# A two-layer hybrid diffusion block in fp32 on one core: norms split in two steps, and four smaller moves

## The chip, the cores and the metric

One core of a Trainium2 chip runs the whole program in one launch. The metric is the device time of that launch in microseconds (us), the median of the runs that were taken; lower is better. Beside the plain runs there is one profiled execution, from which every view below is read: its engines are PE (TensorE, matrix products), PEld (its weight loads), DVE (VectorE), ACT (ScalarE), POOL (GpSimd) and SP (SyncE, which issues the transfers).

## The reference, cut to what matters

Two layers run over 512 latent tokens (LAT below) and 256 context tokens (CTX). Layer 0 computes both streams; layer 1 needs the context only as keys, values and start states, so most of its products have 512 columns alone.

```python
for l in range(DEPTH):                                   # DEPTH = 2
    need_ctx = l < DEPTH - 1
    mod_l = silu_c @ w_ada[l] + b_ada[l]                 # six (1, 1024) vectors
    sh1, sc1, g1, sh2, sc2, g2 = split(mod_l, 6)         # the same for the context
    h_lat = rms_norm(x, norm1_g[l]) * (1 + sc1) + sh1
    h_ctx = ...
    mix_lat, mix_ctx = token_mixing(h_lat, h_ctx, ...)   # w_in, four branches, gates, w_out
    x = x + g1 * mix_lat
    x = x + g2 * swiglu(rms_norm(x, norm2_g[l]) * (1 + sc2) + sh2, w_ffn_in[l], w_ffn_out[l])
    if need_ctx:
        ...                                              # the same two steps for the context
```

The four branches are a diagonal complex state-space layer (S5), a spatial gating unit (SGU), a Mamba-2 mixer with a short convolution (SSD) and multi-head latent attention (MLA). The sizes that count here: w_out is 1024 x 1024, w_ffn_in 1024 x 5632, w_ada 1024 x 6144, all fp32.

## The kernel before, in words

**Layout.** Activations lie with channels on the 128 partitions and tokens along the free dimension; 1024 channels are eight tiles, numbered k. A projection (`proj`, `mm3`) makes one tile of 128 output channels over one segment of tokens (LAT 512 columns, CTX 256). For every k it runs three products, whi with the low part of the activations, whi with the high part, wlo with the high part: fp32 is split into two fp32r numbers, and 24 products make one output tile.

**Weights.** `weights` fetches 256 columns of a weight (1 MB for 1024 rows) into one of two `raw` buffers, and `wsplit` makes two weight tiles of each: ACT casts `whi`, then DVE or POOL subtracts `wlo`. There are two buffers of each of `whi` and `wlo`. The loop over segments in `layer` stands outside the loop over w_out's tiles, so layer 0 fetches and splits w_out twice, once for LAT and once for CTX; layer 1, with LAT alone, once.

**Norms.** `norm_scale` squares the eight tiles on ACT, adds them on DVE, sums over channels and turns tokens onto the partitions with small products with a matrix of ones, takes 1/sqrt in nine tiny DVE steps (`tok_rsqrt`, `rsqrt`), and spreads the result over the partitions again (`bcast_tok`: DVE scales the identity by it, PE multiplies with ones). `norm_mod` then makes from each tile x the modulated high part h (ACT) and low part (DVE and POOL). It is a generator; one `next` emits a whole segment.

**Order.** The Python code emits instructions in the order of the text, with several generators that are stepped by hand; a list scheduler of the framework then orders every engine's queue by priority and readiness, so an instruction may stand far from where the text has it. Each engine runs its queue in order. SP issues all transfers from one queue.

**The places that the change touches.** (1) The start, in `run`: x, eight chunks of w_ada (`ada_first`) and the context are loaded, then w_in's first columns; the LAT norm, the context's transposes (`turn_x`) and norm, and S5's scalar preparation (`s5_scalars`, DVE) come before layer 0's `mix` starts with the q projections, two tiles (`pair`) over LAT and CTX. (2) `layer`, between w_out and the FFN: after the last w_out tile `next(norm)`, then `late`, three chunks of w_ada (`ada_chunk`: 1 MB each, eight products with 32 output rows, a copy and two transposes), then FFN projections, gate and up. (3) The end of layer 0: the last FFN product is followed by layer 1's first norm (`then`). (4) `prepare`, stepped after each of the 22 hidden tiles of layer 0's FFN: w_ada chunks of layer 1 and S5's matrices for it (`s5_prep`). (5) `mla_pair`, the square sums of q and kv. (6) the callback of the convolution in `mix`.

Of the kernel before, what the change touches and what calls it, by code (L numbers as in the profile page):

```python
# [85 lines left out]
class Net:  # L86
# [194 lines left out]
    def bcast_tok(s, r, nb):  # L281
        dg = s.sc()
        for b in range(nb):
            s.ts(dg[:, b * P:(b + 1) * P], s.ident, r[:, b:b + 1])
        ps = s.b1()
        s.mm(ps[:, :nb * P], s.ones, dg[:, :nb * P])
        return ps
# [111 lines left out]
    def ada_first(s, l):  # L399
# [3 lines left out]
        for pool, tag, c, w, cuts in ((s.hp, "h", 0, 768, (0, 512, 768)), (s.hp, "h", 768, 768, (0, 256, 768)), (s.fp, "f", 1536, 512, (0, 512))):  # L403
            rows = []
            for k in range(KD):
# [5 lines left out]
        return out  # L411
# [74 lines left out]
    def norm_scale(s, xs, off, n):  # L486
# [10 lines left out]
        return s.bcast_tok(s.tok_rsqrt(a, n // P, 1.0 / D, 1e-6), n // P)  # L497

    def norm_mod(s, xs, gs, sh, segs, hh, hl, scaled={}):

        for off, n, v in segs:
            sl = slice(off, off + n)
            if off not in scaled:
                rb = s.norm_scale(xs, off, n)
# [142 lines left out]
    def mla_pair(s, part, q, kd, off, t0, b0, xd, nk, nw, wh, wl, qk):  # L647
# [8 lines left out]
        sq, z = s.sc(), s.sc()  # L656
        s.act(sq, x[:, 0:2].rearrange("p k t -> p (k t)"), AF.Square)
        s.add(sq[:, :256], sq[:, :256], sq[:, 256:])
        if nk == 3:
            s.act(z[:, :256], x[:, 2], AF.Square)  # L660
            s.add(sq[:, :256], sq[:, :256], z[:, :256])
# [623 lines left out]
    def mix(s, l, q, xs, xd, hh, hl, segs, rest, ws):  # L1285
# [92 lines left out]
        def conv(c, segs_):  # L1378
# [3 lines left out]
            def cb(ps, off, n, v):  # L1382
                a = y[:, off:off + n]
                s.act(a, ps, AF.Identity, scale=w(1), bias=q["cb"][:, c:c + 1])
                s.stt(a[:, 1:n], ps[:, 0:n - 1], w(0), a[:, 1:n], ALU.mult, ALU.add)
                s.stt(a[:, 0:n - 1], ps[:, 1:n], w(2), a[:, 0:n - 1], ALU.mult, ALU.add)
# [76 lines left out]
    def layer(s, l, q, f, xs, hh, hl, xd, extra, rest, late, then, ws=None):  # L1463
        full = l < DEPTH - 1
        segs = [LAT, CTXS] if full else [LAT]
        yd, gd = s.mix(l, q, xs, xd, hh, hl, segs, rest, ws)
# [20 lines left out]
        for ci, (c0, nc_) in enumerate(chunks):  # L1487
            ah, al = [], []
            for i in range(nc_):
# [144 lines left out]
```

## Time and profile before

| what | value |
|---|---|
| median of 3 runs | 2734.05 us (2726.58 to 2735.45) |
| the profiled execution, its own time | 2746.22 us |
| its span, first to last instruction | 2744.4 us |
| mean granted PE clock in it | 0.978 of full |
| PE busy / PE weight loads busy | 2614.2 us / 2136.0 us |
| DVE, ACT, POOL busy | 1390.6, 959.9, 1217.3 us |
| moved by DMA | 397.31 MB, mean 145 GB/s |

The span is the time from the first instruction to the last; what lies around it in the profiled execution is 1.8 us. The profiled execution is 12.2 us longer than the median of the plain runs. A row of the timeline gives start, duration, engine, source line, what is written from what and shapes; "x3" are three such instructions merged; a bracket gives the engine's idle time just before and what ended it. Tile names: `acc` and `b` PSUM tiles, `xr` x, `raw`, `whi`, `wlo` weights, `h`, `g`, `f` large SBUF tiles, `sc` scratch, `k` the constants with the identity, `mod` and `gs` the modulation vectors (`gs` is also the name of staging tiles).

### The profile page before, as it was taken

To read this page: it belongs to the slowest core of one execution; us is meant where nothing else is said; L and a number is where in the kernel's file an instruction comes from. 1 tells how busy PE (TensorE), PEld (TensorE's weight loads), DVE (VectorE), ACT (ScalarE), POOL (GpSimd) and SP (SyncE) were. 2 spreads that over 40 slices of the span, in tenths; PEclk is the share of its full clock that TensorE was granted. 3 is DMA by queue.
4 is the path that set the end of the run, shared out by engine and by line. 5 is a ranking of instruction groups with operands and counts; after the bars stand their busy time and mean duration, and the time that the engine had idled before them with its cause. 6 is when DMAs were issued, how large, how long until landed. Compare 5 with 4: busy or idle time off the path is not lost. (4 is left out here: it accounts for less than half of the span.)

```text
span 2744.4 us, 39887 instructions
## 1 busy us (share of the span) xinstructions
PE 2614.2 (95%) x14964; PEld 2136.0 (78%) x14964; DVE 1390.6 (51%) x2944; ACT 959.9 (35%) x1901; POOL 1217.3 (44%) x877
## 2 busy tenths in 40 slices
PE   7998999998999989999999989999999999899999
PEld 4787777777888877888888877887766877678887
DVE  6667777656535666552221243666647454421111
ACT  4244455552222233222222234445543233322222
POOL 3255544424433746563423334543224545444443
PEclk9999999999999999999999999999999999899999
DMA  7656645644446553442321334665544565333332
GB/s 254 179 177 196 193 149 164 193 124 149 141 145 215 174 164 118 119 123 71 100 78 55 100 103 156 195 194 179 154 145 151 183 191 188 92 111 93 101 99 77
DMA packets 426039, 397.31 MB, mean 145 GB/s; under 512 B 53092, under 2 KB 372248, under 8 KB 425752
## 3 DMA queue, kind: packets, MB, share of 16 engines
q1 hardware_dynamic: 425848, 394.78, 46.4%
q8 instruction: 118, 1.93, 0.3%
q14 instruction: 73, 0.60, 0.1%
HBM read 305.66 MB, written 89.05 MB: 144 GB/s over the span
## 5 line engine op out<-in xcount | busy, mean ns | idle before, releaser
L174 POOL TENSOR_TENSOR wlo<-raw,whi 128x1024 fp32r<-128x1024 f32 (+2 forms) x314 | 630.1, 2008 | 1040.9 <-ACT whi L169 995.4
L193 PE MATMUL acc<-h,whi 128*128 128x512 f32 (+2 forms) x3496 | 1043.4, 368 | 14.3 <-DVE gs L186 6.7
L193 PE MATMUL acc<-h,wlo 128*128 128x512 f32 (+2 forms) x2060 | 760.1, 369 | 11.7 <-POOL wlo L174 6.5
L193 PEld LDWEIGHTS acc<-h,whi 128*128 128x128 f32 (+1 forms) x3496 | 625.1, 190 | 127.8 <-issue 15.4
L169 ACT CAST whi<-raw 128x1024 fp32r<-128x1024 f32 (+2 forms) x390 | 324.9, 834 | 759.7 <-PE b L193 319.4
L193 PEld LDWEIGHTS acc<-h,wlo 128*128 128x128 f32 (+1 forms) x2060 | 390.9, 190 | 83.7 <-POOL wlo L174 11.7
L193 PE MATMUL acc<-g,whi 128*128 128x512 f32 (+1 forms) x768 | 244.8, 390 | 13.2 <-DVE g L186 6.3
L193 PE MATMUL acc<-f,whi 128*128 128x512 f32 (+1 forms) x600 | 230.6, 394 | 6.4 <-POOL f L174 6.1
L193 PE MATMUL b<-h,whi 128*128 128x256 f32 (+1 forms) x696 | 220.8, 326 | 0.0
L193 PE MATMUL b<-h,wlo 128*128 128x256 f32 (+1 forms) x660 | 216.1, 327 | 3.0 <-POOL wlo L174 3.0
L193 PE MATMUL b<-g,whi 128*128 128x256 f32 (+1 forms) x768 | 197.3, 334 | 1.9 <-ACT whi L169 1.9
L193 PE MATMUL b<-f,whi 128*128 128x256 f32 (+1 forms) x600 | 186.6, 321 | 1.7 <-ACT whi L169 1.7
L193 PE MATMUL b<-g,g 128*64 128x128 f32 (+5 forms) x915 | 183.7, 354 | 0.4 <-DVE g L190 0.3
L193 PEld LDWEIGHTS acc<-g,whi 128*128 128x128 f32 x768 | 139.6, 190 | 43.0 <-ACT whi L169 8.4
L193 PEld LDWEIGHTS b<-g,whi 128*128 128x128 f32 x768 | 136.3, 193 | 24.3 <-ACT whi L169 4.7
L193 PEld LDWEIGHTS b<-g,g 128*128 128x128 f32 (+2 forms) x915 | 124.2, 183 | 24.8 <-issue 14.7
L193 PEld LDWEIGHTS b<-h,whi 128*128 128x128 f32 x696 | 132.0, 191 | 13.5 <-issue 0.2
L186 DVE SCALAR_TENSOR_TENSOR sc<-sc,acc 128x512 f32<-128x512 f32 (+1 forms) x45 | 30.7, 682 | 220.3 <-ACT sc L171 220.3
L193 PEld LDWEIGHTS b<-h,wlo 128*128 128x128 f32 x660 | 126.3, 191 | 16.0 <-POOL wlo L174 4.6
L193 PEld LDWEIGHTS acc<-f,whi 128*128 128x128 f32 x600 | 113.0, 189 | 30.9 <-POOL f L174 7.6
L174 POOL TENSOR_TENSOR g<-sc,g 128x256 fp32r<-128x256 f32 (+2 forms) x81 | 86.6, 1070 | 113.7 <-ACT g L169 86.0
L193 PE MATMUL acc<-g,wlo 128*128 128x512 f32 (+1 forms) x336 | 131.4, 391 | 1.1 <-DVE wlo L174 0.7
(273 smaller groups left out, 3858.5 us busy)
## 6 DMA issues: line engine op xcount, KB each, us to landing
raw<-in_w_in_dram SPq DMA_DIRECT2D x50, 1024.0 KB
raw<-in_w_ffn_in_dram SPq DMA_DIRECT2D x88, 512.0 KB
raw<-in_w_ada_dram SPq DMA_DIRECT2D x40, 1024.0 KB
raw<-in_w_ffn_out_dram SPq DMA_DIRECT2D x36, 512.0 KB
gate<-gs SPq DMA_DIRECT2D x32, 384.0 KB
f<-s5w SPq DMA_DIRECT2D x48, 256.0 KB
raw<-in_w_branch_dram SPq DMA_DIRECT2D x32, 384.0 KB
gs<-gate SPq DMA_DIRECT2D x32, 384.0 KB
```

The source lines that it names most:

```text
L169: s.nc.scalar.copy(out=out, in_=x)
L174: (e or s.nc.vector).tensor_tensor(out=out, in0=a, in1=b, op=op)
L186: s.nc.vector.scalar_tensor_tensor(out=out, in0=a, scalar=sc, in1=b, op0=op0, op1=op1)
L193: s.nc.tensor.matmul(out=out, lhsT=l, rhs=r, start=start, stop=stop)
```

## The change

- `norm_scale` becomes `norm_root`, which stops after 1/sqrt; `norm_mod` yields there, and a second `next` emits the broadcast and the modulation. Callers put other work between the two: in `layer` four w_out tiles of the next segment, and for the last segment the gate and up projections of the first segment; at layer 0's end four w_ffn_out tiles; at the start of each `mix` the q projections of LAT.
- In layer 1 the LAT segment of w_out and of the first FFN tile is cut into two parts of 256 tokens, so w_out is fetched and split twice there too.
- `L8` goes from 21 to 24: no w_ada chunk is left between w_out and the FFN; all sixteen go with the sixteen gate steps of `mix`.
- At the start, w_in's first columns are fetched ahead of the last w_ada piece (chunks 6 and 7), the context's transposes, its norm and `params_more` move behind the first q projection over LAT, and `s5_scalars` behind the q projections.
- `prepare` starts after the fourth hidden tile, with 18 steps for 24.
- `mla_pair` squares into two tiles, one in PSUM, so that each DVE addition reads one operand from PSUM; the convolution's three evacuating instructions get a high priority; `bcast_tok` gives every second scaled identity to ACT.

```diff
     def bcast_tok(s, r, nb):
         dg = s.sc()
         for b in range(nb):
-            s.ts(dg[:, b * P:(b + 1) * P], s.ident, r[:, b:b + 1])
+            if b % 2:
+                s.act(dg[:, b * P:(b + 1) * P], s.ident, AF.Copy, scale=r[:, b:b + 1])
+            else:
+                s.ts(dg[:, b * P:(b + 1) * P], s.ident, r[:, b:b + 1])
...
-    def norm_scale(s, xs, off, n):
+    def norm_root(s, xs, off, n):
...
-        return s.bcast_tok(s.tok_rsqrt(a, n // P, 1.0 / D, 1e-6), n // P)
+        return s.tok_rsqrt(a, n // P, 1.0 / D, 1e-6)
...
             if off not in scaled:
-                rb = s.norm_scale(xs, off, n)
+                root = s.norm_root(xs, off, n)
+                yield
+                rb = s.bcast_tok(root, n // P)
...
-        sq, z = s.sc(), s.sc()
-        s.act(sq, x[:, 0:2].rearrange("p k t -> p (k t)"), AF.Square)
-        s.add(sq[:, :256], sq[:, :256], sq[:, 256:])
+        sq, z, p = s.sc(), s.sc(), s.b1()
+        s.act(z[:, :256], x[:, 0], AF.Square)
+        s.act(p[:, :256], x[:, 1], AF.Square)
         if nk == 3:
-            s.act(z[:, :256], x[:, 2], AF.Square)
-            s.add(sq[:, :256], sq[:, :256], z[:, :256])
+            s.act(z[:, 256:], x[:, 2], AF.Square)
+            s.add(p[:, :256], p[:, :256], z[:, 256:])
+        s.add(sq[:, :256], p[:, :256], z[:, :256])
...
-        pair = [(next(ws), to_dram(dq[c * P:(c + 1) * P], segs)) for c in range(2)]
-        for sg in segs:
+        pair = []
+        for c in range(2):
+            pair.append((next(ws), to_dram(dq[c * P:(c + 1) * P], segs)))
+            s.proj(pair[c][0], hh, hl, segs[:1], pair[c][1])
+            if ctx:
+                next(ctx)
+        for sg in segs[1:]:
             for w, cb in pair:
                 s.proj(w, hh, hl, [sg], cb)
+        if l == 0:
+            s.s5_scalars()
...
-        norm = s.norm_mod(xn, f["gs2"], f["sh2"], segs, hh, hl)
-        for sg in segs:
+
+        parts = segs if full else [(t, 256, segs[0][2]) for t in pieces(segs)]
+        norm = s.norm_mod(xn, f["gs2"], f["sh2"], parts, hh, hl)
+        for sg in parts:
             for o, w in enumerate(s.weights(s.t["w_out"][l], 0, D, e=(s.nc.vector, s.nc.gpsimd))):
                 s.proj(w, mh, ml, [sg], out_cb(o), s.either)
+                if sg is not parts[0] and o == 3:
+                    next(norm)
             next(norm)
...
-                for sg in ([[x] for x in segs] if c == 0 else [segs]):
+                for sg in ([[x] for x in parts] if c == 0 else [segs]):
                     s.proj(wg, hh, hl, sg, gate, s.either)
                     s.proj(wu, hh, hl, sg, up, s.either)
+                    if c == 0 and sg[0] is parts[0]:
+                        next(norm)
                 ah.append(hi)
                 al.append(lo)
-                next(extra, None)
+                if c0 + i > 3:
+                    next(extra, None)
...
                     s.proj(w, ah, al, sg, acc_cb(o), s.either)
+                    if last and full and sg[0] is not segs[0] and o == 3:
+                        then(xn)
...
-            for i in range(24):
-                if i % 3 == 0:
-                    s.ada_chunk(nxt["a"], i // 3)
+            for i in range(18):
+                if i % 2 == 0 and i < 16:
+                    s.ada_chunk(nxt["a"], i // 2)
...
-        next(xt)
-        next(norm)
-        s.params_more(0, q)
-        L8 = 21
-        s.s5_scalars()
+
+        def ctx():
+            next(xt)
+            next(norm)
+            s.params_more(0, q)
+            yield
+            next(norm)
+            yield
+        L8 = 24
```

**Where it moves instructions.** On PE, the change from w_out to the FFN in layer 0. Before (`g`, `f`, `h` are the halves of the activations, `raw` a w_ada chunk, `gs` its copy, `k` the identity, `sc` with `ones` the norm's two small products):

```order
L193 MATMUL b_10923<-h_9121,wlo_10920 128x256
L197 MATMUL acc_11047<-k,gs_11056 128x128 x2
L193 MATMUL acc_11065<-raw_11063,cT 32x256 x8
L193 MATMUL b_10975<-ones,sc_10951 128x128 x2
L197 MATMUL acc_11065<-k,gs_11074 128x128 x2
L197 MATMUL b_11475<-k,h_11465 128x128 x4
L197 MATMUL b_11483<-k,h_11467 128x128 x4
L193 MATMUL acc_11083<-raw_11081,cT 32x256 x8
L197 MATMUL acc_11083<-k,gs_11092 128x128 x2
L193 MATMUL b_10995<-sc_10992,ones 128x256
L193 MATMUL acc_11112<-f_10313,whi_11102 128x512
```

And of the change, the same place, the row behind w_out's last and the rows around the context's broadcast, 52 rows on:

```order
L193 MATMUL b_10989<-h_9187,wlo_10986 128x256
L193 MATMUL acc_11071<-f_10379,whi_11061 128x512
L193 MATMUL acc_11071<-h_10371,whi_11061 128x512
...
L193 MATMUL b_11099<-h_10378,wlo_11066 128x512
L197 MATMUL b_12203<-k,h_12193 128x128 x4
L197 MATMUL b_12211<-k,h_12195 128x128 x4
L193 MATMUL b_11130<-sc_11127,ones 128x256
L193 MATMUL b_12593<-h_12585,ty_12187 16x128 x4
L193 MATMUL b_12605<-h_12586,ty_12188 16x128 x4
L193 MATMUL acc_11180<-f_10387,whi_11061 128x256
```

The w_ada chunks are gone from there; gate and up over LAT, 48 products, stand between w_out's last product and the context's broadcast. S5's transposes and products for layer 1 (`k,h` and `h,ty`) are still there.

The same place in layer 1. Before:

```order
L193 MATMUL b_22973<-h_21992,wlo_22970 128x512
L193 MATMUL acc_23101<-raw_23099,cT 32x256
L193 MATMUL acc_23119<-raw_23117,cT 32x256 x8
L197 MATMUL acc_23101<-k,gs_23110 128x128 x2
L197 MATMUL acc_23119<-k,gs_23128 128x128 x2
L193 MATMUL b_23025<-ones,sc_23001 128x128 x4
L193 MATMUL acc_23137<-raw_23135,cT 32x256 x8
L197 MATMUL acc_23137<-k,gs_23146 128x128 x2
L193 MATMUL b_23049<-sc_23044,ones 128x512
L193 MATMUL acc_23166<-f_22729,whi_23156 128x512
```

Of the change (gate of the first half, the second half's sum, up of the first half, the second half's broadcast, gate of the second half):

```order
L193 MATMUL b_23407<-h_22068,wlo_23404 128x256
L193 MATMUL acc_23489<-f_22805,whi_23479 128x256
...
L193 MATMUL acc_23489<-h_22804,wlo_23480 128x256
L193 MATMUL b_23459<-ones,sc_23435 128x128 x2
L193 MATMUL b_23517<-f_22805,whi_23483 128x256
...
L193 MATMUL b_23517<-h_22804,wlo_23484 128x256
L193 MATMUL b_23548<-sc_23545,ones 128x256
L193 MATMUL acc_23598<-f_22805,whi_23479 128x256
```

w_out there is now 384 products of 256 columns for 192 of 512, in two passes over eight weight tiles each.

On ACT at the start, where h_442 to h_449 are the modulated LAT tiles k = 0 to 7 and `gs_425` the copy of w_ada's chunks 6 and 7. Before:

```order
L171 ACTIVATE h_444<-g_334,mod_205,gs_206 128x512
L171 ACTIVATE h_445<-g_335,mod_205,gs_206 128x512
L171 ACTIVATE h_446<-g_336,mod_205,gs_206 128x512
L171 ACTIVATE sc_478<-g_337,mod_205,gs_206 128x512
L169 COPY g_211<-b_494 128x256
```

Of the change:

```order
L169 CAST whi_173<-raw_171 128x1024
L169 CAST whi_677<-raw_171 128x1024
L171 ACTIVATE h_442<-g_332,mod_205,gs_206 128x512
L171 ACTIVATE sc_462<-g_333,mod_205,gs_206 128x512
L171 ACTIVATE h_443<-g_333,mod_205,gs_206 128x512
L171 ACTIVATE h_444<-g_334,mod_205,gs_206 128x512
L171 ACTIVATE h_445<-g_335,mod_205,gs_206 128x512
L169 COPY gs_425<-acc_415 128x512
```

The first two weight tiles are cast ahead of all of h, where they stood behind most of it, and the copy for chunks 6 and 7 now comes after h's first four tiles.

## Rows read from the trace of the kernel before

**Rows 1.** The page: engine totals, and the granted PE clock in 40 slices.
```profile
PE 2614.2 (95%) x14964; PEld 2136.0 (78%) x14964; DVE 1390.6 (51%) x2944; ACT 959.9 (35%) x1901; POOL 1217.3 (44%) x877
PEclk9999999999999999999999999999999999899999
```

**Rows 2.** Waits of PE, whole span: for whom, us in total, times, longest.
```profile
PE b L193 <- DVE sc L190: 9.4, 4, 3.7
PE acc L193 <- POOL f L174: 6.1, 1, 6.1
PE acc L193 <- DMA raw<-in_w_ada_dram: 5.2, 2, 2.9
```

**Rows 3.** Stretches: length, busy us (count) of PE, PEld, DVE, ACT, POOL; clock; DMA share; GB/s.
```profile
43.90:63.50 19.60, 15.36 (x55) 11.27 (x55) 13.85 (x30) 6.21 (x14) 8.29 (x7) 0.83 0.60 209
987.50:1020.60 33.10, 28.86 (x219) 26.39 (x218) 27.56 (x51) 17.56 (x26) 21.04 (x13) 0.95 0.44 140
1020.60:1036.30 15.70, 7.25 (x50) 4.71 (x51) 14.34 (x28) 4.65 (x8) 12.57 (x10) 0.70 1.00 309
1036.30:1040.60 4.30, 4.30 (x15) 2.58 (x14) 4.27 (x6) 0.60 (x1) 3.15 (x3) 0.51 0.53 127
2297.30:2346.30 49.00, 47.66 (x214) 36.22 (x218) 19.86 (x23) 12.72 (x17) 14.40 (x6) 1.00 0.40 126
2346.30:2363.60 17.30, 7.33 (x46) 3.24 (x38) 11.63 (x30) 5.41 (x9) 5.91 (x3) 0.64 0.74 208
2363.60:2368.40 4.80, 4.78 (x11) 3.69 (x12) 4.30 (x7) 2.83 (x4) 2.66 (x3) 0.51 0.49 131
```

**Rows 4.** Timeline of PE, layer 0: a w_ada chunk, and the context's broadcast.
```profile
1016.44 1.07 PE L193 MATMUL acc<-raw,cT 128*32 128x256 f32 x16
...
1035.68 1.22 PE L193 MATMUL b<-sc,ones 128*128 128x256 f32 x2 [3.75 <-DVE sc L190]
```

**Rows 5.** Timeline of DVE, layer 0: the two scaled identities of that broadcast.
```profile
1032.22 3.41 DVE L190 TENSOR_SCALAR sc<-k,ty 128x128 f32<-128x128 f32 x2
```

**Rows 6.** Timeline of PE: first and last of 18 products of 256 columns, of 14 of 512.
```profile
999.75 0.28 PE L193 MATMUL b<-g,whi 128*128 128x256 f32 x1
...
1001.79 0.28 PE L193 MATMUL b<-h,wlo 128*128 128x256 f32 x1
...
2329.68 0.39 PE L193 MATMUL b<-h,whi 128*128 128x512 f32 x1
...
2332.62 0.39 PE L193 MATMUL b<-h,wlo 128*128 128x512 f32 x1
```

**Rows 7.** Waits of PE in 987.5 to 1020.6, the context's w_out pass.
```profile
PE acc L193 <- DVE wlo L174: 2.0, 2, 1.2
PE b L193 <- POOL wlo L174: 1.8, 1, 1.8
```

**Rows 8.** Timeline of SP's queue: w_out's last three transfers of layer 0.
```profile
979.91 0.38 SPq L527 DMA_DIRECT2D raw<-in_w_out_dram  x1
...
991.21 0.39 SPq L527 DMA_DIRECT2D raw<-in_w_out_dram  x1
...
998.93 0.38 SPq L527 DMA_DIRECT2D raw<-in_w_out_dram  x1
```

**Rows 9.** Timeline of PE: LAT's broadcast at the end of layer 0.
```profile
1632.70 1.13 PE L193 MATMUL b<-sc,ones 128*128 128x512 f32 x2 [2.94 <-DVE sc L190]
```

**Rows 10.** Timeline of PE at the start: first products over LAT, and over CTX.
```profile
43.89 2.08 PE L193 MATMUL acc<-h,whi 128*128 128x512 f32 x4 [0.33 <-POOL h L174]
...
63.47 0.51 PE L193 MATMUL acc<-h,whi 128*128 128x256 f32 x2 [2.17 <-POOL h L174]
```

**Rows 11.** DVE's square-sum additions: MLA's by group in 100 to 320, timeline of a norm's.
```profile
L174 DVE TENSOR_TENSOR sc<-sc 128x256 f32<-128x256 f32 x6 | 5.6, 928 | 5.0 <-ACT sc L171 5.0
...
50.65 3.11 DVE L174 TENSOR_TENSOR b<-b,sc 128x256 f32<-128x256 f32 x6
```

**Rows 12.** Timeline of PE: the product that waits for MLA's square sum.
```profile
166.30 0.86 PE L193 MATMUL b<-ones,sc 128*128 128x128 f32 x4 [2.58 <-DVE sc L174]
```

More of the change, by code (lines that the diff above doesn't have):

```diff
@@ L397, in ada_load, with ada_first @@
         return [raw[:, j] for j in range(KD)]
-    def ada_first(s, l):
+    def ada_first(s, l, between):
         src = s.t["w_ada"][l].rearrange("(k p) f -> p k f", p=P)
@@ L404, in ada_first @@
             rows = []
+            if tag == "f":
+                done = between()
             for k in range(KD):
@@ L410, in ada_first @@
                 out.append(((c + a) // 256, b - a, [x[:, a:b] for x in rows]))
-        return out
+        return out, done
     def ada_chunk(s, a, i, w=256, raw=None):
@@ L1282, in s5_glu, with mix @@
             yield
-    def mix(s, l, q, xs, xd, hh, hl, segs, rest, ws):
+    def mix(s, l, q, xs, xd, hh, hl, segs, rest, ws, ctx):
         t = s.t
@@ L1383, in cb @@
                 a = y[:, off:off + n]
-                s.act(a, ps, AF.Identity, scale=w(1), bias=q["cb"][:, c:c + 1])
-                s.stt(a[:, 1:n], ps[:, 0:n - 1], w(0), a[:, 1:n], ALU.mult, ALU.add)
-                s.stt(a[:, 0:n - 1], ps[:, 1:n], w(2), a[:, 0:n - 1], ALU.mult, ALU.add)
+                with s.tc.high_priority(2000):
+                    s.act(a, ps, AF.Identity, scale=w(1), bias=q["cb"][:, c:c + 1])
+                    s.stt(a[:, 1:n], ps[:, 0:n - 1], w(0), a[:, 1:n], ALU.mult, ALU.add)
+                    s.stt(a[:, 0:n - 1], ps[:, 1:n], w(2), a[:, 0:n - 1], ALU.mult, ALU.add)
                 z = s.sc()[:, :n]
@@ L1461, in merge, with layer @@
         return mh, ml
-    def layer(s, l, q, f, xs, hh, hl, xd, extra, rest, late, then, ws=None):
+    def layer(s, l, q, f, xs, hh, hl, xd, extra, rest, late, then, ws=None, ctx=None):
         full = l < DEPTH - 1
         segs = [LAT, CTXS] if full else [LAT]
-        yd, gd = s.mix(l, q, xs, xd, hh, hl, segs, rest, ws)
+        yd, gd = s.mix(l, q, xs, xd, hh, hl, segs, rest, ws, ctx)
         mh, ml = s.merge(l, yd, gd, segs)
@@ L1543, in run @@
         xr = s.load_x()
-        chunks = s.ada_first(0)
+        ws = s.weights(s.t["w_in"][0], C_CQ, BR)
+        chunks, first = s.ada_first(0, lambda: next(ws))
         xr = s.load_ctx() + xr
-        ws = s.weights(s.t["w_in"][0], C_CQ, BR)
-        first = next(ws)
         q = turn({})
@@ L1553, in run @@
         off, n, _ = LAT
-        rb = s.norm_scale(xs, off, n)
+        rb = s.bcast_tok(s.norm_root(xs, off, n), n // P)
         xl = [s.g()[:, :n] for _ in range(KD)]
@@ L1596, in then, with ctx1 @@
             next(nxt["norm"])
-        s.layer(0, q, a["f"], xs, hh, hl, xd, ex, rest(a, 8, L8), rest(a, L8, 24), then, chain([first], ws))
+        def ctx1():
+            yield
+            next(nxt["norm"])
+            yield
+        s.layer(0, q, a["f"], xs, hh, hl, xd, ex, rest(a, 8, L8), rest(a, L8, 24), then, chain([first], ws), ctx())
         xd = [s.dram(f"x1_{k}", [P, TOK]) for k in range(KD)]
-        s.layer(1, nxt["q"], nxt["a"]["f"], nxt["x"], *nxt["h"], xd, iter(()), rest(nxt["a"], 8, L8), rest(nxt["a"], L8, 24), None)
+        s.layer(1, nxt["q"], nxt["a"]["f"], nxt["x"], *nxt["h"], xd, iter(()), rest(nxt["a"], 8, L8), rest(nxt["a"], L8, 24), None, None, ctx1())
 @with_exitstack
```

## The prediction

> **What bounds the kernel now.** I read the page first [rows 1]: PE is busy 95% of the span, its own weight loads 78% and no other engine over 51%, so PE sets the end, and the change can win only where PE waits or runs at its lower clock. The 40 slices of the clock read 9 in all but one, so such places are short. I took PE's waits next, by whom it waited for [rows 2], and picked the entries with few, long waits: the norm's scaled identity (`sc` of line 190, 9.4 us in 4 waits), one wait of 6.1 us for a half of the FFN's input made on POOL, and 5.2 us for two w_ada transfers. The reader is to see single places there, not a rate. Last I cut out the stretches around these places [rows 3]: from w_out's last product to the FFN's first it takes 15.70 us in layer 0 with PE busy 7.25, and 17.30 us in layer 1 with 7.33 busy; the granted clock is 0.70 and 0.64 there, and 0.51, the lower level of 1.2 GHz, for the FFN's first 4.3 and 4.8 us. What PE did before each fall was to wait for half of the time.
>
> **The change part by part.** All sums are against the profiled execution's own 2746.2 us; the median of the plain runs, 2734.05, is 12.2 us lower, and I take the difference over to it unchanged.
>
> *Layer 0, w_out to FFN.* The stretch of 15.70 us [rows 3] closes, as gate and up over LAT need nothing of the context's norm. Not all of it is idle: 7.25 us of PE work at clock 0.70 are 7.25 x 0.70 = 5.1 us at full clock (w_ada chunks, S5's products, the norm's small ones), and those stay, here or in `mix`. A chunk costs PE about 1.1 us [rows 4]. Saved are 15.7 - 5.1 = 10.6 us, and 4.3 x 0.49 = 2.1 us of the half clock behind it, 12.7 together. What is late next is the context's own norm. Its way took the 15.7 us; now it has 48 products of 512 columns for cover, at (2332.62 - 2329.68) / 13 = 0.226 us from start to start [rows 6], 10.8 us. PE's queue is in order, so behind the context's broadcast the whole FFN waits. The rest of the way, 4.9 us, is the upper bound of the new wait, and 0 the lower, since the w_ada transfer that took part of the 15.7 is gone. But S5's work for layer 1 still stands there in the order, and with it two scaled identities took 3.41 us [rows 5], so I take 3. **Term -10, between -13 and -8.**
>
> *Layer 1, w_out to FFN.* By the same sum the stall gives 17.3 - 7.33 x 0.64 = 12.6 us and the half clock 4.8 x 0.49 = 2.4 [rows 3], 15.0 together. Three costs stand against it. First the second half's norm: its cover is 48 products of 256 columns at 2.04 / 17 = 0.120 us [rows 6], 5.8 us; the way of a norm of 256 columns is at most layer 0's 15.7, so the wait lies between 0 and 9.9. No S5 work is here (POOL was busy 5.91 us of the stall, against 12.57), so I take 3. Second, 48 FFN products of 512 columns become 96 of 256: 48 x (0.240 - 0.226) = 0.7 us. Third, and largest, w_out in two passes of 256 columns. If PE alone counted, they would take 384 x 0.120 = 46.1 us, where the pass now takes 49.0 less two w_ada chunks of 1.1, 46.8: a gain of 1. The nearest row is layer 0's pass over the context, the same shape and code: 33.1 us for 192 products [rows 3], with 3.8 us of waits for `wlo` [rows 7], one chunk (1.1) and clock 0.95. Less the chunk that is 32.0, and two of them cost 64 - 47 = 17. Which end is nearer? In that pass DVE was busy 27.56 and POOL 21.04 of 33.1 us, with LAT's whole norm and S5's matrices; in layer 1 a norm of half the width competes alone, and DVE and POOL had 19.86 and 14.40 us in 49.0 [rows 3]. On the other side PE is done with a 1 MB pair of weight tiles after 48 x 0.120 = 5.8 us, and the transfers came 7.7 and 11.3 us apart [rows 8], through two buffers. At 7 us a pair a pass takes 28, two take 56: cost 9, in the middle, and I take that. **Term -15.0 + 3 + 0.7 + 9 = -2, between -15 and +13.**
>
> The narrower product itself is in those passes: 192 x (0.240 - 0.226) = 2.7 us by [rows 6]. The Trainium skill, page "TensorE: Matmul & The Clock Gate", section "Back-to-back issue gap", gives columns / 2.4 + 2.5 ns from start to start when warm, an estimate of 109 and 216 ns, by which halving costs 0.4 us, and the term would be 2 us better.
>
> *End of layer 0.* LAT's broadcast makes PE wait 2.94 us [rows 9]. With four w_ffn_out tiles in between it is hidden; the waits for weights around it stay. **Term -3, between -3 and 0.**
>
> *Start.* The first product over LAT starts at 43.89, the first over CTX at 63.47 [rows 10]; in between PE is busy 15.36 of 19.6 us at clock 0.83 [rows 3]. Now the weights come first, so products can start with h's first four tiles, 24 of them, at most 24 x 0.226 = 5.4 us earlier. But ACT, in order, casts both weight tiles ahead of h; chunks 6 and 7 of w_ada come 1 MB later, which at 209 GB/s [rows 3] is 5.0 us; and the context's sum now follows all LAT products, with nothing behind it but its own broadcast, where today one of the two tiles covers it. The gain is bounded by the 5.4 and by all idle time and lost clock up to the first CTX product, 19.6 - 15.36 x 0.83 = 6.9 us; the loss by the 5.0. I take a little gain, as cover is both won and lost. **Term -2, between -12 and +5.**
>
> *MLA's square sums.* q's pair makes two additions of 0.93 us each; the norms' additions with an operand in PSUM take 3.11 / 6 = 0.52 [rows 11], so the chain to the product that waits 2.58 us [rows 12] is 0.8 us shorter, in two layers 1.6. At most both waits go, 2 x 2.58. **Term -1.6, between -5 and 0.**
>
> *At nothing.* MLA's extra ACT square and PSUM buffer: ACT is busy 35% [rows 1]; without that cover the square costs the chain about what the additions give. The w_ada chunks in the gate steps, and `s5_scalars` later: PE has 48 or more products per step to hide a 1 MB transfer; without that cover there is a wait as now, 5.2 us for two [rows 2]. The scaled identities on ACT, the convolution's priority and the later `prepare`: no long wait of [rows 2] ends on what they move, once the broadcasts are hidden. The scheduler redoes all queues, for which there is no row; I allow 5 us to either side.
>
> Sum: -10 - 2 - 3 - 2 - 1.6 = -19 us, so 2734 - 19 = **2715 us**.
>
> **The rivals.**
>
> *The half passes are free.* w_out in layer 1 runs at PE's pace: the third cost is -1 for 9, the sum -29, the time 2705 us. For it speaks the emptier DVE and POOL [rows 3]; against it, that every second `wlo` comes from POOL and that the context's pass waited for just those [rows 7].
>
> *The weights eat what the norms give.* Two passes as slow as in layer 0 (17 for 9), the context's norm at its upper bound (4.9 for 3) and nothing at the start (0 for -2): -19 + 8 + 2 + 2 = -7 us, 2727 us, no measurable change. For it: this is the pass as measured, and S5's work still stands beside the context's norm. Against it: the emptier engines.
>
> *Slower: the second reading of w_out.* If the eight transfers in layer 1 come at the longer spacing of [rows 8], 11.3 us, the passes take 90 us and cost 43 for 9; the sum is -19 + 34 = +15, the time 2749 us. It decides from 9.4 us per transfer on (75 us for eight, cost 28). For it: a buffer comes free only behind POOL's subtraction, and x is loaded through the same queue. Against it: the other spacing was 7.7, and DMA moved 140 GB/s there, against 309 in the stretch behind [rows 3]. The Trainium skill, page "TensorE: Matmul & The Clock Gate", section "HAM oscillation — how this bites in real kernels", speaks for it: where the work on one weight tile is shorter than the wait for the next, PE drops to its lower clock time and again. By that rule both passes would run partly at half clock. The context's pass, at 0.95 [rows 3], bears it out in a small part.
>
> **How the numbers follow.** A difference under 0.3% (8 us) can hardly be told from none here. The forecast gets 0.55, the free passes 0.15, the weights that eat it 0.17, the slower case 0.13. Faster is the first two, 0.70; same 0.17; slower 0.13. The range leaves out no more than 2 in 10: downward the free passes with 10 us for the start and the reordering, upward the case without change, with the bounds of layer 1 beyond it, to just under the break-even plus 8: 2694 to 2741.
>
> **What would show it.** In the profile after: the FFN's first product within 2 us of w_out's last in both layers, at full clock; one wait for the second norm under 5 us, some 11 us later in layer 0 and some 6 us later in layer 1; two w_out passes in layer 1 of about 28 us each with transfers 7 us apart; no wait for w_ada; a first LAT product before 43 us and a first CTX product near 61. I am wrong if those passes take over 32 us each, if the context's norm outlasts its cover by more than 5 us, or if stretches that are only reordered (MLA, attention, S5) move by more than 5 us.

## The result, and the profile after

The kernel after takes **2764.93 us** (median of 4 runs, 2760.93 to 2769.2) against 2734.75 for before beside it: ratio **1.0119, 95% interval 1.0102 to 1.0136**, 30 us slower, where 19 us faster was forecast. The profiled execution takes 2769.2 us. On the page, PE stays the bound and its clock is no worse (the lines of [rows 1]):

```profile
PE 2621.2 (95%) x15206; PEld 2150.6 (78%) x15206; DVE 1402.2 (51%) x2980; ACT 978.4 (35%) x1951; POOL 1226.7 (44%) x888
...
PEclk9999999999999999999999999999999999999999
```

Next come the waits of PE over the whole span (for whom, us in total, times, longest). The scaled identities, w_ada and the FFN input of [rows 2] are gone from the head of the list. The waits for PSUM tiles to be copied out (`gs`) have grown, a wait for S5's `h` has come, and the norms' sums (`sc` of line 174) make fewer waits but a longer one. The kernel after, then the same rows of the kernel before:

```profile
PE acc L193 <- DVE gs L186: 12.5, 9, 5.3
PE acc L193 <- ACT gs L171: 11.3, 9, 2.9
...
PE b L193 <- DVE sc L174: 5.3, 4, 4.2
...
PE b L193 <- DVE h L186: 4.4, 2, 3.7
```
```profile
PE b L193 <- DVE sc L174: 9.9, 7, 2.6
...
PE acc L193 <- DVE gs L186: 6.7, 5, 3.1
...
PE acc L193 <- ACT gs L171: 4.7, 2, 3.8
```

To see where the time went, I cut both traces at equal PE work: products are summed in PE's order, each weighed with the usual spacing of its shape, and a cut stands where the sum is the same. So a stretch holds the same amount of work in every kernel, and where work was moved, as the w_ada chunks were, the cut falls at another place of the program; around w_out such a cut is good to some 3 us, an estimate from other weights for the products. The profile of [rows 1 to 12] came from an execution 12 us above the median; for this I use a second profile of before (run e5, 2735.0 us). First that kernel, then the one after (columns as in [rows 3]; MLA of layer 0, its last gates and w_branch, w_out to the second hidden tile, end of layer 0, MLA and attention of layer 1, its w_out to the second hidden tile):

```profile
199.20:658.40 459.20, 435.02 (x2846) 350.68 (x2842) 334.72 (x760) 220.87 (x530) 208.60 (x174) 0.97 0.56 169
...
784.50:983.90 199.40, 195.04 (x1082) 167.83 (x1082) 105.84 (x164) 59.07 (x109) 92.70 (x73) 1.00 0.56 175
983.90:1080.50 96.60, 81.94 (x525) 68.00 (x524) 77.17 (x137) 40.40 (x74) 68.01 (x48) 0.91 0.51 155
...
1595.60:1675.80 80.20, 69.25 (x368) 54.67 (x367) 47.13 (x101) 38.33 (x66) 35.52 (x27) 1.00 0.48 151
1675.80:2122.80 447.00, 436.30 (x2649) 343.53 (x2648) 270.80 (x619) 203.05 (x446) 175.24 (x135) 0.98 0.55 173
...
2286.50:2388.80 102.30, 90.05 (x399) 67.35 (x398) 43.01 (x67) 30.80 (x43) 39.71 (x21) 0.92 0.37 114
```
```profile
199.40:675.90 476.50, 443.13 (x2834) 354.00 (x2833) 342.40 (x758) 221.85 (x536) 201.61 (x171) 0.97 0.54 162
...
800.40:1006.20 205.80, 197.69 (x1121) 167.57 (x1121) 107.10 (x172) 59.62 (x111) 92.71 (x73) 1.00 0.58 184
1006.20:1106.00 99.80, 80.52 (x477) 70.17 (x476) 78.58 (x123) 41.19 (x72) 67.91 (x48) 0.93 0.37 112
...
1620.40:1696.90 76.50, 68.97 (x356) 54.82 (x355) 49.15 (x95) 38.51 (x66) 34.80 (x26) 1.00 0.47 147
1696.90:2156.40 459.50, 438.27 (x2655) 343.46 (x2654) 263.99 (x619) 206.32 (x453) 175.62 (x135) 0.98 0.54 169
...
2318.20:2422.10 103.90, 92.49 (x599) 83.50 (x598) 52.91 (x107) 44.75 (x72) 54.85 (x35) 0.95 0.45 138
```

The reader is to see the first column after the window: MLA +17.3, gates +6.4, w_out to FFN +3.2 (forecast -10), end of layer 0 -3.7 (-3), layer 1's MLA and attention +12.5, its w_out to FFN +1.6 (-2). The two large losses lie in stretches whose work the change hardly touches. The second has to be read with care: the first profile of before takes 454.0 us there for the 447.0 of the second. The same cut for all runs that the argument needs (us):

```
                    e5 before  after    e1     e6     e7     e8     e9    e10    e12    e13
start                   194.9  195.3  194.4  193.4  192.9  194.1  191.9  191.3  193.7  192.0
MLA 0                   459.2  476.5  459.6  472.8  464.1  456.4  460.8  457.7  458.8  459.6
attention 0             126.1  124.5  126.1  124.5  123.9  126.1  126.1  126.1  126.1  126.1
gates, w_branch 0       199.4  205.8  207.4  199.7  205.4  200.6  206.7  200.8  200.7  205.1
w_out to FFN 0           96.6   99.7  101.7   96.2  101.4   97.0   85.4   97.0   95.4   85.2
FFN 0                   515.1  514.4  511.1  513.7  512.9  513.9  515.0  513.8  513.3  514.4
end of layer 0           80.2   76.5   76.4   82.1   76.5   77.8   76.3   77.8   80.7   81.0
MLA, attention 1        447.0  459.5  458.9  446.9  453.2  462.5  458.8  457.9  447.0  448.9
gates, w_branch 1       163.7  161.8  162.2  169.6  163.1  163.4  161.6  163.9  164.3  163.3
w_out to FFN 1          102.3  103.9  102.1  102.5  101.1  101.2  102.3  102.4  101.1  101.3
```

### The profile page after: what moved, and what is told of

Same layout as the page of the kernel before. It is cut to its first block, busy times and chain, and to the rows that moved or that the text cites. A ratio compares the mean times of both kernels' runs of the same rounds, so it can differ in the third digit from the quotient of the medians.

```text
span 2767.1 us, 40538 instructions
## 1 busy us (share of the span) xinstructions
PE 2621.2 (95%) x15206; PEld 2150.6 (78%) x15206; DVE 1402.2 (51%) x2980; ACT 978.4 (35%) x1951; POOL 1226.7 (44%) x888
## 5 line engine op out<-in xcount | busy, mean ns | idle before, releaser
L174 POOL TENSOR_TENSOR wlo<-raw,whi 128x1024 fp32r<-128x1024 f32 (+2 forms) x318 | 639.9, 2013 | 1060.5 <-ACT whi L169 1011.7
L193 PE MATMUL acc<-h,whi 128*128 128x512 f32 (+2 forms) x3536 | 1057.8, 367 | 24.2 <-DVE gs L186 12.5
L193 PE MATMUL acc<-h,wlo 128*128 128x512 f32 (+2 forms) x2100 | 768.1, 366 | 10.9 <-POOL wlo L174 6.8
L193 PEld LDWEIGHTS acc<-h,whi 128*128 128x128 f32 (+1 forms) x3536 | 634.6, 191 | 139.9 <-issue 16.2
L169 ACT CAST whi<-raw 128x1024 fp32r<-128x1024 f32 (+2 forms) x398 | 333.4, 838 | 754.3 <-PE b L193 325.5
L193 PEld LDWEIGHTS acc<-h,wlo 128*128 128x128 f32 (+1 forms) x2100 | 400.1, 191 | 79.2 <-POOL wlo L174 10.7
L193 PE MATMUL b<-h,wlo 128*128 128x256 f32 (+1 forms) x700 | 224.7, 321 | 6.0 <-POOL wlo L174 6.0
L193 PE MATMUL b<-h,whi 128*128 128x256 f32 (+1 forms) x736 | 228.5, 319 | 0.0
L193 PEld LDWEIGHTS b<-h,whi 128*128 128x128 f32 x736 | 140.8, 193 | 11.9
L193 PEld LDWEIGHTS b<-h,wlo 128*128 128x128 f32 x700 | 134.8, 193 | 18.2 <-POOL wlo L174 8.7
```

Of the source, the lines that this page charges most:

```text
L169: s.nc.scalar.copy(out=out, in_=x)
L174: (e or s.nc.vector).tensor_tensor(out=out, in0=a, in1=b, op=op)
L193: s.nc.tensor.matmul(out=out, lhsT=l, rhs=r, start=start, stop=stop)
```

## The experiments

Four theories stood at the start. Theory A: the square sums slow MLA. Theory B: the late `s5_scalars` crowd S5's work into it. Theory C: no single edit does it, but the new order as a whole. Theory D: S5's work for layer 1 stands in the way of layer 0's second norm. Times are medians, ratios to before on the same chip; a line `...` marks what is left out of an edit.

**e1, e2, e3, e4: one edit of the kernel after undone each.**

```diff
# e1: the sums of mla_pair as before
-        sq, z, p = s.sc(), s.sc(), s.b1()
-        s.act(z[:, :256], x[:, 0], AF.Square)
-        s.act(p[:, :256], x[:, 1], AF.Square)
...
+        sq, z = s.sc(), s.sc()
+        s.act(sq, x[:, 0:2].rearrange("p k t -> p (k t)"), AF.Square)
...
# e2
-                with s.tc.high_priority(2000):
# e3
-        L8 = 24
+        L8 = 21
# e4: from mix to run, ahead of it
-            s.s5_scalars()
+        s.s5_scalars()
         ex = prepare()
```

> The kernel after, with the square sums of q's and kv's pairs as before (one wide square on ACT, the additions from SBUF). Theory A, the new sums are what slows the MLA stretches (layer 0 about 313 to 676 us, layer 1 about 1836 to 2006 us, together some 31 us longer than before): this kernel is 20 to 30 us faster than the kernel after, near 2738. Theory B, the late S5 scalars crowd the S5 work into layer 0's MLA stretch: within 5 us of the kernel after, 2760 to 2770. Theory C, no single edit does it and the scheduler's order as a whole does: 0 to 10 us faster, with the gain somewhere other than in MLA.

Measured: 2750.86 us, 1.0069 (1.0054 to 1.0084), 0.5% or 14 us under the kernel after. Layer 0's MLA is back (459.6 us), layer 1's is not (458.9): theory A holds for the one and not for the other, and gives 14 us where it had 20 to 30.

> The kernel after, with the convolution's three evacuating instructions at their old priority. Theories A and B: within 5 us of the kernel after, as the convolution stands behind the MLA stretch (676 to 800 us), which is even 1.6 us shorter than before. Theory C: up to 10 us to either side, in stretches that hold no convolution. Rival: the priority shifts ACT and DVE in layer 1's attention, and the 9 us there come back.

Measured: 2767.86 us, 1.0127 (1.0112 to 1.0143), no difference from the kernel after.

> The kernel after, with three w_ada chunks of each layer between w_out and the FFN again. If the chunks in the gate steps cost nothing, as predicted: the three chunks (3.3 us of PE work) hide beside the products there, the time is within 4 us of the kernel after. If they are what lengthens the stretch of the last gates and w_branch (about 800 to 905 us, 7.8 us longer than before, with three waits of PE at the chunks' transposes): that stretch is 5 to 8 us shorter, as much of it in layer 1, and the time 5 to 12 us below the kernel after.

Measured: 2776.41 us, 1.0172 (1.0155 to 1.0189), 11 us slower than the kernel after. By the same cut the gates are back at 199.7 us, but w_out to FFN takes 106.6 and, in layer 1, 112.5. So moving the chunks is a gain in all.

> The kernel after, with S5's scalar preparation ahead of the mixing again. Theory B: layer 0's MLA stretch (313 to 676 us, 22 us longer than before) gives back 10 to 20 us, at the price of up to 3 us at the start; the time is near 2750. Theory A: within 4 us of the kernel after. Layer 1's MLA stretch (9 us longer than before) stays as it is under both.

Measured: 2805.5 us, 1.0265 (1.0245 to 1.0285). Theory B fails: MLA gives back 5 us (471.1), the start takes 37.5 more (232.8). The timeline of PE shows where:

```profile
96.49 1.22 PE L193 MATMUL b<-ones,sc 128*128 128x128 f32 x4 [34.71 <-DVE sc L174]
```

The context's norm is emitted late now; with S5's scalars ahead of it on DVE, PE's queue waits 34.7 us for that norm's sum. The late place of `s5_scalars` is not a free edit: the late context norm needs it.

**e5: before again; e6: before with the sums alone; e7: the kernel after with `p` in scratch.**

```diff
# e7
-        sq, z, p = s.sc(), s.sc(), s.b1()
+        sq, z, p = s.sc(), s.sc(), s.sc()
```

> The kernel before once more, for a second profile: its first one was taken in an execution 12 us longer than the median of the plain runs. If those 12 us lie in one stretch, that stretch will be shorter here by about as much and the stage table against the kernel after moves there; if they are spread, every stretch is shorter by 0.3 to 0.5%.

Measured: 2735.0 us. Of the 11.3 us between the two profiles' spans 6.7 lie between the end of layer 0 and layer 1's w_out; the rest is spread. Layer 1's MLA and attention thus differ by 7 us between two executions of one kernel.

> The kernel before with the new square sums of q and kv alone. Theory A, the sums slow the MLA stretch wherever they stand: 10 to 17 us slower than before, near 2745, with layer 0's stretch from 320 to 660 us longer by 15 to 22 us and a wait or two ahead of it shorter by up to 6. Rival: they cost only together with the other edits: within 4 us of before. As predicted (the terms of the sum as they were): 1.6 us faster, no slower than before.

Measured: 2754.78 us, 1.0077 (1.0057 to 1.0097): 21 us slower than before by this edit alone: 13.6 of it in layer 0's MLA, and 5.9 in layer 1's last gates (169.6 for 163.7), which the full change does not show.

> The kernel after, with the second square tile of q and kv in SBUF scratch and not in PSUM; the narrow squares and the chain of additions stay. If the PSUM buffer, one of four that S5, MLA and attention share, is what moves the MLA stretch: 10 to 15 us faster than the kernel after, near 2751. If the narrower squares on ACT or the mere reordering are: within 4 us of the kernel after. If scratch (five buffers) becomes the scarce one: slower than the kernel after.

Measured: 2751.76 us, 1.0062 (1.0041 to 1.0083). The squares stay narrow and the additions in two tiles; only the PSUM buffer is gone, and 13 us are back. So the buffer is the cause. What it holds up is read from the rows of one tile, kv's second step on DVE (`kd`; min/median/max ns, first and last start), in e5, the kernel after and e7:

```profile
L174 DVE TENSOR_TENSOR g<-kd,ty x6: 345/352/1207, 272.6 to 316.7; 128x192 f32<-128x192 f32 x6
```
```profile
L174 DVE TENSOR_TENSOR g<-kd,ty x6: 339/346/1218, 282.1 to 342.3; 128x192 f32<-128x192 f32 x6
```
```profile
L174 DVE TENSOR_TENSOR g<-kd,ty x6: 351/352/2503, 270.8 to 317.1; 128x192 f32<-128x192 f32 x6
```

The three pairs of kv spread over 60 us for 44 in e5 and 46 in e7, and their last steps fall into S5's and the next projections' work. There the copies out of PSUM (`gs<-gs,acc`) stand behind them on DVE. PE's next product waits 5.32 us and starts as the second of these copies ends (324.00 + 0.67). This is the longest of several such waits; the others were not followed one by one, and that this path makes up the whole of the 13 us is not shown. DVE, then PE, of the kernel after:

```profile
316.35 1.49 DVE L174 TENSOR_TENSOR g<-kd,ty 128x192 f32<-128x192 f32 x2
...
317.89 1.42 DVE L174 TENSOR_TENSOR f<-ty,f 128x512 f32<-128x512 f32 x1
319.23 1.80 DVE L174 TENSOR_TENSOR g<-g,ty 128x384 f32<-128x384 f32 x2
...
321.43 0.68 DVE L186 SCALAR_TENSOR_TENSOR gs<-gs,acc 128x512 f32<-128x512 f32 x1
322.03 1.78 DVE L174 TENSOR_TENSOR f<-f,f 128x512 f32<-128x512 f32 x1
...
324.00 0.67 DVE L186 SCALAR_TENSOR_TENSOR gs<-gs,acc 128x512 f32<-128x512 f32 x1
```
```profile
324.73 1.22 PE L193 MATMUL acc<-h,whi 128*128 128x512 f32 x2 [5.32 <-DVE gs L186]
```

**e8: old sums, and layer 0 as before. e9: old sums, S5 held back.**

```diff
# e8, on e1: layer 0's norm in one step, three chunks late, prepare as before
             next(norm)
+            if full:
+                next(norm)
...
-        s.layer(0, q, a["f"], xs, hh, hl, xd, ex, rest(a, 8, L8), rest(a, L8, 24), then, chain([first], ws), ctx())
+        s.layer(0, q, a["f"], xs, hh, hl, xd, ex, rest(a, 8, 21), rest(a, 21, 24), then, chain([first], ws), ctx())
...
# e9, on e1: behind the first hidden tile
+                if full and c0 + i == 0:
+                    for _ in range(8):
+                        s.act(s.h()[:, :1], hi[:, :1].bitcast(F32))
```

> The kernel after with the square sums as before, and in layer 0 the norm behind w_out in one step, three w_ada chunks there, and 24 preparation steps from the first hidden tile on, all as before; layer 1's halves, the start, the end of layer 0 and the small edits stay. Theory D, splitting layer 0's norm gained nothing since S5's work for layer 1 then stands in the FFN's way: 5 to 10 us faster than the kernel with the sums back (2751), near 2743, with 53 and 44 us in the two stretches around the norm where the split kernel has 41 and 61. Theory E, the split was worth the predicted 10 us and other stretches lost: 8 to 12 us slower than that kernel.

Measured: 2749.08 us, 1.0057 (1.0038 to 1.0077). Against e1 layer 0's gates take 6.8 us less and w_out to FFN 4.7, by the profile; the median moves by 2, within the noise. So the split gained nothing in that place, against theory E, and taking it out gives less than the 5 to 10 us that theory D had.

> The kernel after with the old square sums, plus one thing: the eight h tiles that w_out frees in layer 0 pass through a one-column copy that needs the first hidden tile's result, so S5's work for layer 1, which takes these tiles, can start only a hidden tile later. Theory D (S5's matrices on DVE stand ahead of the norm's additions, its products on PE ahead of the context's gate and up): the stretch from w_out's last tiles over the first hidden tile, 40.6 + 61.0 us with the sums back, falls by 8 to 15 us, the norm's sum no longer waits over 1 us for DVE, and the time is 5 to 15 us under 2751. Rival (the norm's own chain outlasts its cover even without S5): within 4 us of 2751, the wait for the sum still 2.5 us or more. Second rival: S5's work is late then and makes PE wait further on in the FFN by as much as it gave.

Measured: 2737.85 us (10 runs), 1.0021 (1.0006 to 1.0037): 13 us under e1, w_out to FFN 85.4 us for 101.7. This is theory D; of its second rival, S5's work waiting further on, some 4 us hold (FFN 0 takes 515.0 us for 511.1). The kernel after, DVE behind w_out's last product (1039.33), then PE from that product on:

```profile
1039.84 3.83 DVE L174 TENSOR_TENSOR h<-sx 128x384 f32<-128x384 f32 x2
1043.58 1.77 DVE L174 TENSOR_TENSOR h<-ty,sx 128x512 f32<-128x512 f32 x1
...
1048.47 2.57 DVE L174 TENSOR_TENSOR b<-b,sc 128x256 f32<-128x256 f32 x5
1051.14 0.42 DVE L174 TENSOR_TENSOR sc<-b,sc 128x256 f32<-128x256 f32 x1
```
```profile
1039.33 0.28 PE L193 MATMUL b<-h,wlo 128*128 128x256 f32 x1
1039.44 0.40 PE L193 MATMUL acc<-f,whi 128*128 128x512 f32 x1
...
1051.62 1.02 PE L193 MATMUL b<-ones,sc 128*128 128x128 f32 x4 [4.16 <-DVE sc L174]
...
1060.12 0.60 PE L193 MATMUL b<-sc,ones 128*128 128x256 f32 x2
...
1064.43 1.03 PE L193 MATMUL b<-h,ty 128*16 128x128 f32 x8 [3.71 <-DVE h L186]
...
1067.90 0.58 PE L193 MATMUL acc<-f,whi 128*128 128x256 f32 x1
```

The FFN starts right behind w_out, so the stall is closed. But S5's `h<-sx` and `h<-ty,sx` go ahead of the norm's additions, the sum comes 4.16 us late behind half of its cover, and S5's own products, which wait 3.71 us, stand ahead of the context's gate: it starts 7.2 us after the broadcast's end (1060.72). In e9 the additions follow at once, the sum and the broadcast wait for nothing, and one long wait is left, 3.03 us behind the broadcast:

```profile
1025.75 2.03 DVE L174 TENSOR_TENSOR b<-b,sc 128x256 f32<-128x256 f32 x4
1027.89 0.42 DVE L174 TENSOR_TENSOR sc<-b,sc 128x256 f32<-128x256 f32 x1
```
```profile
1029.47 0.60 PE L193 MATMUL b<-ones,sc 128*128 128x128 f32 x4
...
1035.37 0.60 PE L193 MATMUL b<-sc,ones 128*128 128x256 f32 x2
...
1039.00 0.38 PE L193 MATMUL acc<-f,whi 128*128 128x256 f32 x1 [3.03 <-POOL f L174]
```

**e10 to e12: why layer 1's MLA and attention are longer.** Theory F: layer 1's own edits do it. e11 is e8 with layer 1's context norm finished at the end of layer 0; e10 moreover has layer 1 in one piece with its chunks late; e12 is e10 without the split of LAT's norm there.

```diff
# e10, e11, on e8
                 if last and full:
                     then(xn)
+                    if sg[0] is not segs[0]:
+                        then(xn)
...
# e10
-        parts = segs if full else [(t, 256, segs[0][2]) for t in pieces(segs)]
+        parts = segs
...
# e12, on e10
-                    if last and full and sg[0] is not segs[0] and o == 3:
-                        then(xn)
                 if last and full:
                     then(xn)
-                    if sg[0] is not segs[0]:
-                        then(xn)
+                    then(xn)
```

> Only three parts of the change are left: the start (weights first, the context's norm and S5's scalars behind the first q products), the split of layer 1's first norm at the end of layer 0 for its LAT half, and the small edits (scaled identities on ACT, the convolution's priority); everything else as before, in layer 1 too. Predicted terms: start -2, end of layer 0 -3. Theory F, the 14 us that layer 1's MLA and attention are longer come from layer 1's own edits: near 2727, a little faster than before. Rival, they come from the small edits: 8 to 14 us slower than that, with layer 1's MLA and attention (163 + 148 us before) still 8 us or more longer.

> The kernel with layer 0 as before (2749), and layer 1's context norm finished at the end of layer 0 again and not behind layer 1's first q products; halves and w_ada chunks of layer 1 as in the kernel after. If the late context norm is what shifts layer 1's MLA and attention: those two stretches (171 + 150 us, 163 + 148 us in the second profile of before) come back, 6 to 12 us faster than 2749, and the end of layer 0 gives back 2 us. If the w_ada chunks or the halves shift them: within 4 us of 2749.

Measured: e10 2743.34 us, 1.0036 (1.0024 to 1.0049); e11 2743.08, 1.0037 (1.0024 to 1.0051). Layer 1's MLA and attention stay at 457.9 us in e10, so theory F falls, and at 460.7 in e11, so the late context norm isn't it. Why e11's median is 6 us under e8's, the stretches don't say: the two profiled executions are 0.5 us apart.

> The kernel with only the start, the end-of-layer-0 split and the small edits left (2743), now also without that split: layer 1's first norm goes in one step per segment again, right behind w_ffn_out. Theory G, the split is what reorders layer 1's MLA and attention: these two stretches come back to within 2 us of before (163 + 148 us), layer 1's norm costs its 3 to 4 us again, and the time is 6 to 12 us under 2743, near 2733. Rival, the small edits or the start do it: both stretches stay 6 us or more longer and the time is 2743 to 2748.

Measured: 2733.07 us (10 runs), 1.0001 (0.9991 to 1.001), 10 us under e10. This is theory G: the split over four w_ffn_out tiles gains 2.9 us where it stands (77.8 for 80.7) and costs 10.9 in layer 1's MLA and attention. One pair of profiles would prove little in that stretch, where two of before differ by 7 us; it is the medians that carry it, 10.3 us here and, by the same edit, 7.9 from e9 to e13. The windows of e10 and e12:

```profile
1668.60:2126.50 457.90, 439.29 (x2654) 343.03 (x2653) 267.74 (x619) 205.60 (x448) 177.00 (x135) 0.99 0.55 169
```
```profile
1672.90:2119.90 447.00, 433.33 (x2649) 340.34 (x2648) 272.21 (x619) 203.36 (x445) 174.28 (x135) 0.99 0.55 173
```

**e13: e9 with e12's edit. e14: e13 with three chunks of layer 0 late.** In e13 `then(xn)` stands twice behind each segment of the last w_ffn_out, as in e12; e14 adds the chunk line of e8:

```diff
-        s.layer(0, q, a["f"], xs, hh, hl, xd, ex, rest(a, 8, L8), rest(a, L8, 24), then, chain([first], ws), ctx())
+        s.layer(0, q, a["f"], xs, hh, hl, xd, ex, rest(a, 8, 21), rest(a, 21, 24), then, chain([first], ws), ctx())
```

> The kernel with S5 held back behind the first hidden tile (2738), without the split of layer 1's first norm. Theory G: 4 to 10 us faster, near 2731, level with before or a little under it, layer 1's MLA and attention (171 + 148 us) 8 us shorter. Rival: the halves and w_ada chunks of layer 1 reorder them as well; then within 3 us of 2738.

Measured: **2729.98 us** (10 runs), **0.9982 (0.9968 to 0.9996)**: faster than both kernels, than before by 0.18%, less than the 0.3% that the prediction calls hardly told from none. In its profile w_out to FFN is 11.4 us shorter than in e5 and the start 2.9, and the gates take 5.7 of that back.

> The kernel of the run before this one (S5 held back, first norm of layer 1 in one step), with three w_ada chunks of layer 0 behind w_out again, where the first segment's gate and up now lie beside them. If the three chunks in the last gate steps are what makes the stretch there longer (102 against 97 us): 4 to 6 us shorter there, and at most 4 us of it lost again between w_out and the second hidden tile; 0 to 6 us faster in all, near 2728. Rival: the chunk's transfers and transposes make PE wait between w_out and FFN as before, and it is 2 to 8 us slower.

Measured: 2734.97 us, 1.0009 (0.9999 to 1.002), 5 us over e13, as the rival had it: the gates give 4.5 us back (200.6), w_out to FFN loses 9.8 (95.0).

## Why the prediction was wrong

**The step that failed** is the last of "At nothing": "The scheduler redoes all queues, for which there is no row; I allow 5 us to either side." Two edits that I had priced at their own place moved the order of long stretches elsewhere, by 14 and 11 us, and both into a loss. It is the last of the conditions that the prediction names for being wrong: stretches that are only reordered moved by more than 5 us. Beside it one term was mis-sized, that of S5's work between w_out and the FFN in layer 0. By the cut at equal work, MLA of layer 0 missed its share of the forecast by 18 us, layer 1's MLA and attention by 13, w_out to FFN of layer 0 by 13 and its gates by 6, of 53 between the two profiles.

*MLA's square sums* (forecast -1.6, between -5 and 0; the PSUM buffer at nothing). Measured +14 (e1) and +21 (e6). I costed the additions and the square, and not the buffer: `pb1` has four, and S5, MLA and attention live on them. The Trainium skill, page "Perfetto Trace Analysis", section "Optimization Strategy", says that repeated gaps on the engine that should be full can mean too little SBUF or PSUM for the next tile to be allocated. The runs agree on the cause, as 13 us are back with one tile in scratch instead, but not on the sign: the waits are single ones of different length, the longest 5.32 us. Why the order comes out so is the scheduler's, and no run shows it.

*End of layer 0* (forecast -3). The wait of [rows 9], 2.94 us, is now 0.56:

```profile
1653.54 1.10 PE L193 MATMUL b<-sc,ones 128*128 128x512 f32 x2 [0.56 <-DVE sc L190]
```

That term was right (-3.7 measured), and its sequel, some 10 us in layer 1, was nowhere in the sum.

*Layer 0, w_out to FFN* (forecast -10, between -13 and -8). Measured +3.2 at equal work; PE is idle 14.7 us of the stretch before and 19.3 after. By the place in the program, from w_out's first product over the context to the second hidden tile, it takes 92.6 us before and 90.7 after, 1.9 less, where the four chunks that left it (three of layer 0, one of layer 1) are 4.3 us of PE work by [rows 4]. I had seen that S5's work stands there, and gave it 3 us, counted from two identities. The stall of before wasn't only the norm's wait: S5 ran in it. With the stall closed, S5 waits in the FFN's queue instead, and it costs 4.16 us ahead of the sum and 4 more ahead of the context's gate. With S5 held back the stretch is 11.2 us shorter than before: the mechanism was right, and the step "with it two scaled identities took 3.41 us [rows 5], so I take 3" mis-sized. That the wait left there is 3.03 us is luck: it is for the context's first tile from POOL, and not for scaled identities.

*Chunks in the gate steps* (at nothing). The gates' stretch is 6.4 us longer at equal work, and 4.5 to 7 us in each pair of runs that differ in the place of the chunks; what waits there was not followed, so the cause stays open. Even so the move gains 5 us in all by e14.

*Layer 1, w_out to FFN* (forecast -2, between -15 and +13). Measured +1.6. The two passes, from the first to the third row below, take 58.1 us where I had 56, the transfers come (2363.7 - 2315.4) / 7 = 6.9 us apart where I had 7, and the second half's wait is 2.32 where I had 3:

```profile
2322.05 0.39 PE L193 MATMUL acc<-g,whi 128*128 128x256 f32 x1 [0.17 <-ACT whi L169]
...
2380.16 0.28 PE L193 MATMUL acc<-f,whi 128*128 128x256 f32 x1
...
2389.55 0.39 PE L193 MATMUL acc<-f,whi 128*128 128x256 f32 x1 [2.32 <-POOL f L174]
```

The slower rival, the second reading of w_out, did not come about: the time came out on its side for other reasons. The granted clock over this stretch is 0.95, against 0.92 before. The rule of the Trainium skill that was weighed for this rival (page "TensorE: Matmul & The Clock Gate", section "HAM oscillation — how this bites in real kernels": PE drops to the lower clock where work on a weight tile is shorter than the wait for the next) was not put to the test: the transfers came 6.9 us apart and PE had 5.8 us of work in between, so it waited for less time than it worked.

*Start* (forecast -2). Measured +0.4 after; runs with the same start lie between -3.6 (e10) and +0.4, and one with the old start (e6) at -1.5, so the term can't be told from nothing. The first LAT product came at 41.02 (43.89 in [rows 10]), the first CTX product at 63.30 (63.47): what was won went to a small transpose in PE's queue ahead of the context's broadcast that waits for a load, and to the wait for h behind it.

```profile
59.65 0.29 PE L197 MATMUL b<-k,sc 34*128 34x34 f32 x1 [3.25 <-DMA sc<-in_sgu_ln_b_dram]
```

## What to carry to other kernels

Before a stall is closed, list what runs in it: that work needs a new place too, and here only the buffers it takes moved it, not a later place in the code (S5's work stood in the FFN's way although `prepare` begins four tiles later). Where a scheduler orders the queues, price an edit by the pools and the ready times it changes, not only by its instructions, and compare the order of the long stretches behind it before believing a sum of local terms. Where edits lean on each other (the late context norm, the late S5 scalars), one without the other can cost more than both bring: 40 us here.

## What the runs showed of the hardware

I had not expected how long plain DVE instructions last beside POOL. In the kernel after, the modulation of a 128x512 tile on DVE takes 0.67 us at 1039.24, where another POOL instruction is about to end, and 2.38 where POOL's weight subtraction (2.40) began just before it; S5's next `h<-sx` stands beside a second one (2.52). Over the whole trace five such modulations with no POOL instruction beside them take 0.53 to 0.55 us, and five that start while POOL subtracts weights 0.82 to 2.58. POOL, then DVE:

```profile
1034.25 2.40 POOL L174 TENSOR_TENSOR wlo<-raw,whi 128x1024 fp32r<-128x1024 f32 x1
...
1039.59 2.52 POOL L174 TENSOR_TENSOR wlo<-raw,whi 128x1024 fp32r<-128x1024 f32 x1
...
1044.77 1.51 POOL L174 TENSOR_TENSOR h<-ty,sx 128x512 f32<-128x512 f32 x1
```
```profile
1034.55 2.38 DVE L190 TENSOR_SCALAR sc<-sc,gs,mod 128x512 f32<-128x512 f32 x1
...
1039.24 0.67 DVE L190 TENSOR_SCALAR sc<-sc,gs,mod 128x512 f32<-128x512 f32 x1
...
1045.28 0.42 DVE L174 TENSOR_TENSOR b<-b,sc 128x256 f32<-128x256 f32 x1
```

So the subtraction that was handed to POOL to spare DVE takes DVE's time as well, where DVE works on SBUF tiles alone. The last row of each shows the other case: the norms' additions, with an operand in PSUM, last 0.43 us in the median both with no POOL instruction beside them (10) and with one running as they start (25). MLA's old additions of the same size, from scratch tiles, take 0.42 us with none beside them in e5 (1), and 0.41 to 1.69, 1.03 in the median, with one running as they start (10). The 0.93 us that the prediction set against 0.52 is thus largely the price of working beside POOL, and not of the addition itself.
